# A list scheduler's prices for TensorE: new durations and a new charge for changes of tiling

## The chip, the cores and the metric

The kernel runs on one core of one Trainium2 chip. The metric is the device time of one execution in microseconds. One execution more was profiled; all durations below come from it. TensorE (PE) multiplies matrices, PEld is its loading of the stationary operand, DVE is VectorE, ACT is ScalarE, POOL is GpSimd, SP is SyncE, which issues the DMAs.

## The reference, cut to what matters

Four transformer layers on 512 tokens of width 1024, everything in float32. The first two layers each run four mixers side by side (a gated linear attention with 64-wide heads, `hgrn2`; one with 32-wide keys, `gla`; a causal softmax attention, `mla`; a gated delta rule, `gdn`) and then a feed-forward part with a gated, convolved projection. The last two are an attention layer with differences of softmaxes and a stick-breaking layer, both with a small attention over 256 memory tokens.

```python
def first_block(x, ...):
    for l in range(DEPTH):
        z = rms_norm(x, pre_mix_g[l]) @ w_in[l]            # 512 x 3256
        o_a = hgrn2_mixer(...)     # chunk_gla, chunks of 64, 4 heads of 64
        o_b = gla_mixer(...)       # chunk_gla, keys of 32
        o_c = mla_mixer(...)       # causal softmax
        o_d = gdn_mixer(...)       # chunk_gated_delta: triangular solve, then 8 chunks in sequence
        mix = jnp.concatenate([o_a, o_b, o_c, o_d], axis=-1) @ w_out[l]
        x = x + rms_norm(mix, post_mix_g[l])
        x = x + rms_norm(conv_glu_ffn(rms_norm(x, pre_ffn_g[l]), ...), post_ffn_g[l])   # 1024 -> 2816 -> 1024
    return x

def reference(...):
    return second_block(first_block(x, ...), ...)   # diff attention layer, stick-breaking layer
```

## The kernel before

The large products (projections, feed-forward, output projections) are done with float32 split into a high and a low `fp32r` part, three matmuls for one (`mm3`, L814). These are 128x128 tiles of the array with 256 to 512 moving columns, and they are called dense below. The small products of the mixers are plain float32: of 64 rows and 64 columns (K = 64, M = 64, n = 64) in `gdn` (L1540) and parts of `gla_core` (L1072), of 128 rows and 64 columns in the six levels of `gla_core`, a few with 32. A plain float32 matmul is two MATMUL instructions in the profile. In `gdn` they come in batches of 32 matmuls (`batch`, L1624) that read tiles which DVE or ACT has just written; the eight chunks in sequence come as groups of four.

No instruction is issued while the Python program runs. Every call of an engine is put down as an `Op` in a `Plan` (L261) with what it must follow, and `Plan.emit` (L324) issues them at the end in the order that `Plan.order` (L410) returns. This is why L328 is the line of every row of the profile. The order comes from a list scheduler, `Plan.simulate` (L422). It holds a clock for each engine. Whenever an engine is free on that clock it takes, of the ops that are ready, the one with the lowest rank (the place in which the Python program wrote it, as far as tiles suffice: `feasible`, L378), and moves the clock on by the op's price, `Plan.cost` (L330). A successor on another engine becomes ready at the end plus a hop (`HOP`). The start times of this simulation, sorted (L595), are the instruction order of every engine's queue and of the DMA queue. On the chip each queue then runs strictly in that order and waits on semaphores: prices only decide the order.

Four things in `simulate` touch PE alone:

- the price of a matmul by its type, K, M and n (L333 to L343);
- the tiling: if an op's pair of K and M, each cut off at 64, isn't that of the op before, 0.08 us are added (L555). By that cut, 128x128, 128x64 and 64x64 are one class;
- a guess of the TensorE clock: if too few columns were streamed in a period of the model, prices double in the next (`slow`, L500, L562);
- mixing (L505 to L534): if few columns have lately been streamed (`lately`, `MIX`, `CHUNK`), ops with `dense` below 0.9 are passed over as long as a denser one is ready. `dense` is an op's columns per ns of its price (L414), so a price can move an op over that bound.

All 8 PSUM banks are in three pools: `psA` for the projections, `psS` and `psD` for the mixers.

Of the kernel before, what the change touches and what calls it, by code (L numbers as in the profile page):

```python
# [164 lines left out]
class Clocks:  # L165
# [20 lines left out]
    def cost(self, e, kind, outs, ins):  # L186
        n = max(_free(a) for a in outs + ins)
        if e == "PE":
            if kind == "transpose":
                return 0.105  # L190
            n = _free(ins[-1])
            return max(0.055, n / 2400) if ins[-1].dtype == F32R else max(0.085, n / 600)
        if e == "ACT":
            return 0.2 + 0.83e-3 * n
        if e == "DVE":
            return 0.15 + (0.52e-3 if kind in ("tensor_scalar", "tensor_copy", "memset") else 1.04e-3) * n
        if e == "POOL":
            return 0.2 + 2.2e-3 * n
        return 2.5
# [61 lines left out]
class Plan:  # L261
# [68 lines left out]
    def cost(self, op):  # L330

        n = max([_free(a) for a in op.outs] + [_free(a) for a in op.ins])
        psum = any(a.tensor.name.startswith("ps") for a in op.ins)  # L333
        if op.eng == "PE":
            if op.kind == "transpose":
                return 0.11
            n = _free(op.ins[-1])
            if op.ins[-1].dtype == F32R:
                return 0.0025 + max(n, 256) / 2400
            M = op.outs[0].shape[0]  # L340
            if M > 64:
                return max(0.214, 0.002 + n / 600)
            return 0.0135 + n / 1200 if M <= 32 else max(0.081, 0.028 + n / 1200)  # L343
        if op.eng == "ACT":
            acc = 0.1 if op.kw.get("accum_out") is not None else 0.0
            ptr = any(hasattr(op.kw.get(k), "tensor") for k in ("scale", "bias"))
            return (0.05 if psum else 0.09) + 0.833e-3 * n + acc + (0.09 if ptr else 0.0)
        if op.eng == "DVE":
            if op.kind == "reciprocal":
                return 0.07 + 6.25e-3 * n  # L350
            if op.kind == "memset":
                return 0.01 + 1.042e-3 * n
            fast = op.kind in ("tensor_scalar", "tensor_copy") and not psum
            ptr = any(hasattr(op.kw.get(k), "tensor") for k in ("scalar", "scalar1", "scalar2"))
            return 0.07 + (0.521e-3 if fast else 1.042e-3) * n + (0.06 if ptr else 0.0)
        if op.eng == "POOL":
            if op.kw.get("op") == ALU.pow:
                return 0.3 + 0.165 * _free(op.outs[0])
            return 0.15 + (2.1e-3 if op.kind == "tensor_tensor" else 3.33e-3) * n
        return 0.45  # L360
# [4 lines left out]
    TABLES = {AF.Exp: "natural_log_exp_and_others", AF.Ln: "natural_log_exp_and_others", AF.Silu: "silu",  # L365
              AF.Sigmoid: "sigmoid", AF.Gelu_apprx_tanh: "gelu", AF.Sin: "sin"}
    TABLE_LOAD = 1.3

    WINDOW, COLUMNS = 10.24 / 3, 3060.0
    MIX, CHUNK = 1.2, 1000.0  # L370
# [48 lines left out]
    def hop(self, a, b):  # L419
        return self.HOP.get((a, b), 0.1)  # L420

    def simulate(self, rank, prio):  # L422
# [60 lines left out]
        indeg = [len(op.preds) for op in ops]  # L483
        at = [0.0] * len(ops)
        table, bw = None, 0.0
        cols, window, slow, boost, tiling = 0.0, 0, True, False, None
        recent, lately = collections.deque(), 0.0
        events = []
        for op in ops:
# [5 lines left out]
        while len(out) < len(ops):  # L495
            t, e = heapq.heappop(events)
            if clock[e] > t:
                continue
            while e == "PE" and t >= (window + 1) * self.WINDOW:
                slow = cols < self.COLUMNS  # L500
                cols, window = 0.0, window + 1
            while later[e] and later[e][0][0] <= t:
                _, n = heapq.heappop(later[e])
                heapq.heappush(ready[e], (prio[n], n))
            pick, skipped = None, []  # L505
            if e == "PE":
                while recent and recent[0][0] < t - self.WINDOW:
                    lately -= recent.popleft()[1]
                boost = lately < self.MIX * self.COLUMNS + (self.CHUNK if boost else 0.0)
            while ready[e]:  # L510
                p, n = heapq.heappop(ready[e])
                op = ops[n]
                wait, tag = None, None
                for nm in op.new:
                    tag = self.tags[nm][0]
                    if not free[tag] or not can(nm):
                        wait = math.inf
                        break
                    if free[tag][0] > t:
                        wait = free[tag][0]  # L520
                        break
                if wait is not None:
                    if wait < math.inf:
                        heapq.heappush(later[e], (wait, n))
                    else:
                        blocked.setdefault(tag, []).append(n)
                    continue
                if e == "ACT" and op.func in self.TABLES and self.TABLES[op.func] != table and at[n] + self.PATIENCE > t:
                    skipped.append((p, n))
                    continue  # L530
                if boost and op.dense < 0.9 and e == "PE":
                    skipped.append((p, n))
                    continue
                pick = n  # L534
                break
            if pick is None and skipped:
                pick = skipped.pop(0)[1]
            for x in skipped:
                heapq.heappush(ready[e], x)
            if pick is None:  # L540
                if later[e]:
                    heapq.heappush(events, (max(later[e][0][0], t + 1e-6), e))
                continue
            op = ops[pick]
            start = t
            wake = set()
            for nm in op.new:
                take(nm)
                wake.add(self.tags[nm][0])
            if e == "ACT" and op.func in self.TABLES and self.TABLES[op.func] != table:  # L550
                table = op.table = self.TABLES[op.func]
                start += self.TABLE_LOAD
            op.start = start
            if e == "PE":
                mode = min(op.ins[0].shape[0], 64), min(op.outs[0].shape[0], 64)  # L555
                cost = op.cost * (2 if slow else 1) + (0.08 if mode != tiling else 0.0)
                tiling = mode
                cols += self.columns(op)
                lately += self.columns(op)
                recent.append((start + cost, self.columns(op)))  # L560
                while start + cost >= (window + 1) * self.WINDOW:
                    slow = cols < self.COLUMNS  # L562
                    cols, window = 0.0, window + 1
            else:
                cost = op.cost
            clock[e] = end = start + cost
            if e == "DMA":
                n = 4e-6 * math.prod(op.outs[0].shape)
                bw = end = max(bw, start + 1.8) + n / 0.36
                end += 0.9  # L570
            op.end = end
            out.append(op)
            for nm in op.tiles:
                left[nm] -= 1
                tend[nm] = max(tend[nm], end)
                if not left[nm]:
                    drop(nm, tend[nm] + 0.15)
                    wake.add(self.tags[nm][0])
            for tag in wake:
                for n in blocked.pop(tag, ()):  # L580
                    f = ops[n].eng
                    heapq.heappush(later[f], (t, n))
                    heapq.heappush(events, (max(t, clock[f]), f))
            for s in op.succs + op.soft:
                f = ops[s].eng
                if s in op.succs:
                    at[s] = max(at[s], end + hop(e, f))
                else:
                    at[s] = max(at[s], start + 0.01)
                indeg[s] -= 1  # L590
                if not indeg[s]:
                    heapq.heappush(later[f], (at[s], s))
                    heapq.heappush(events, (max(at[s], clock[f]), f))
            heapq.heappush(events, (clock[e], e))
# [19 lines left out]
class Net:  # L614
# [256 lines left out]

    def fm(self, h, w, M=128):

        ps = self.ps("A")
        for k in range(KT):
            self.mm3(ps[:M], (w[0][:, k, :], w[1][:, k, :]), self.hp(h, k, 0, S), k == 0, k == KT - 1)
        return ps
# [66 lines left out]

    def w_fm(self, W, c0, M=128):
        return self.wload(self.cols(W, c0, M))

# [1576 lines left out]
```

## Time and profile before

| | us |
|---|---|
| three runs: median (lowest to highest) | 2035.56 (2032.98 to 2035.82) |
| the profiled execution: its time | 2033.99 |
| its span, first to last instruction | 2032.2 |
| PE busy in it | 1954.1 (96%) |
| DVE / ACT / POOL busy | 1250.3 / 946.6 / 265.7 |
| mean granted TensorE clock | 0.987 |

The stretches: mixers of the first layer from about 60 to 260 us, of the second from 784 to 984; feed-forward from about 380 to 735 and from 1100 to 1450; the attention layers from 1450 to the end. In a timeline row, start and length are in us, equal instructions that follow each other are merged (x is their number), and the brackets give the engine's idle time before them and what ended it. A length includes the way through the array, so rows overlap: the pace of a group is the distance of starts.

### The profile page before, as it was taken

How to read it: one execution, taken by the hardware profiler on the slowest of the kernel's cores; microseconds unless marked ns; L12 is line 12 of the kernel's file. 1: busy time of each engine (PE TensorE's matmuls, PEld its weight loads, DVE VectorE, ACT ScalarE, POOL GpSimd, SP SyncE). 2: the span in 40 equal slices, each digit the busy share in tenths (PEclk: the TensorE clock that was granted, in tenths of full speed). 3: DMA queues.
4: the chain of work that ended last, by engine and by line, in shares of the span. 5: the costliest groups of instructions: out<-in, count | busy, mean ns of one | idle time of the engine just before them, and what ended most of it. 6: DMA issues, size and time to landing. Idle time of an engine off the chain costs nothing.

```text
span 2032.2 us, 33173 instructions
## 1 busy us (share of the span) xinstructions
PE 1954.1 (96%) x13254; PEld 1655.6 (81%) x13254; DVE 1250.3 (62%) x2319; ACT 946.6 (47%) x1715; POOL 265.7 (13%) x362
## 2 busy tenths in 40 slices
PE   7999989899999989998898999999999999999999
PEld 6888778788888878887787888888899988888787
DVE  7688873544442257878836444422548886558796
ACT  5744463433332236633634333322446774457782
POOL 3101111000000021011201000000223220005131
PEclk9999989999999999999999999999999999999999
DMA  5321224433332433302243333324331213421121
GB/s 166 97 63 36 83 81 138 125 94 94 98 99 94 155 90 96 92 24 68 82 152 112 100 94 94 99 97 167 121 89 43 84 63 114 135 84 55 60 74 62
DMA packets 231305, 191.62 MB, mean 94 GB/s; under 512 B 22352, under 2 KB 201200, under 8 KB 231152
## 3 DMA queue, kind: packets, MB, share of 16 engines
q1 hardware_dynamic: 231152, 189.51, 30.4%
q8 instruction: 104, 1.70, 0.3%
q14 instruction: 49, 0.40, 0.1%
HBM read 174.28 MB, written 15.20 MB: 93 GB/s over the span
## 4 chain that ended last, share of the span: by engine, by line
PE 84%; DVE 7%; ACT 3%; POOL 2%; issue 2%; DMA 1%; SPq 1%; DVEq 0%; ACTq 0%; POOLq 0%
PE psA L328 63%; PE psS L328 12%; PE psD L328 9%; DVE p4w L328 5%; POOL st L328 2%; ACT p4w L328 1%; DVE p4p L328 1%; DVE wl L328 1%; SPq L328 1%; DVE p L328 1%; ACT wh L328 0%; DMA wr<-in_w_in_dram 0%; ACT p4p L328 0%; ACT p L328 0%; DVE p4h L328 0%
## 5 line engine op out<-in xcount | busy, mean ns | idle before, releaser
L328 PE MATMUL psA<-p4h,wh 128*128 128x512 f32 (+1 forms) x2144 | 627.9, 377 | 14.3 <-DVE p4h L328 7.1
L328 DVE TENSOR_TENSOR wl<-wr,wh 128x1024 fp32r<-128x1024 f32 (+6 forms) x304 | 349.0, 1152 | 413.7 <-ACT wh L328 408.4
L328 ACT CAST wh<-wr 128x1024 fp32r<-128x1024 f32 (+6 forms) x304 | 298.5, 990 | 465.2 <-PE psA L328 279.8
L328 PEld LDWEIGHTS psA<-p4h,wh 128*128 128x128 f32 x2144 | 393.5, 191 | 89.9 <-DVE p4h L328 8.3
L328 PE MATMUL psA<-p4h,wl 128*128 128x512 f32 (+1 forms) x1072 | 400.6, 374 | 0.0
L328 PE MATMUL psA<-wh,p4h 128*128 128x256 f32 (+1 forms) x1792 | 353.8, 289 | 0.9 <-DVE p4h L328 0.7
L328 PEld LDWEIGHTS psA<-wh,p4h 128*128 128x128 f32 x1792 | 282.3, 188 | 6.6 <-issue 2.0
L328 PE MATMUL psA<-wl,p4h 128*128 128x256 f32 (+1 forms) x896 | 257.5, 288 | 0.4 <-DVE wl L328 0.4
L328 PEld LDWEIGHTS psA<-p4h,wl 128*128 128x128 f32 x1072 | 204.3, 191 | 37.0
L328 POOL TENSOR_SCALAR st<-st 128x1 f32<-128x1 f32 (+4 forms) x108 | 46.1, 427 | 1310.6 <-ACT p4w L328 908.5
L328 PEld LDWEIGHTS psA<-wl,p4h 128*128 128x128 f32 x896 | 168.8, 188 | 2.6 <-DVE wl L328 0.8
L328 PE MATMUL psA<-wh,p4w 128*128 128x512 f32 (+1 forms) x540 | 159.4, 368 | 0.0
L328 ACT ACTIVATE p<-p 128x512 f32<-128x512 f32 (+2 forms) x174 | 87.3, 526 | 100.2 <-DVE p L328 98.9
L328 POOL TENSOR_TENSOR st<-st,c 128x1 f32<-128x1 f32 (+4 forms) x106 | 115.4, 1090 | 8.0
L328 ACT ACTIVATE p4w<-psA 128x256 f32<-128x256 f32 (+5 forms) x138 | 61.6, 452 | 107.0 <-PE psA L328 105.9
L328 PEld LDWEIGHTS psA<-wh,p4w 128*128 128x128 f32 x540 | 96.6, 188 | 18.2 <-issue 0.5
L328 PE MATMUL psS<-consts,p4w 128*128 128x128 f32 (+1 forms) x448 | 70.5, 291 | 36.7 <-DVE p4w L328 28.9
L328 PE MATMUL psS<-p4w,p4w 128*64 128x64 f32 (+9 forms) x800 | 94.6, 271 | 5.3 <-DVE p4w L328 5.1
L328 PE MATMUL psA<-wl,p4w 128*128 128x512 f32 (+1 forms) x270 | 98.5, 365 | 0.0
L328 PE MATMUL psS<-wh,p4w 128*128 128x512 f32 x300 | 97.3, 395 | 0.0
L328 DVE TENSOR_TENSOR p<-psA,p 128x512 f32<-128x512 f32 x54 | 37.3, 691 | 95.8 <-PE psA L328 94.2
L328 PEld LDWEIGHTS psS<-consts,p4w 128*128 128x128 f32 x448 | 54.5, 153 | 47.7 <-issue 19.1
(227 smaller groups left out, 3105.0 us busy)
## 6 DMA issues: line engine op xcount, KB each, us to landing
wr<-in_w_in_dram SPq DMA_DIRECT2D x44, 512.0 KB, 3.8
wr<-in_ffn_w_gate_dram SPq DMA_DIRECT2D x44, 512.0 KB, 3.8
wr<-in_ffn_w_up_dram SPq DMA_DIRECT2D x44, 512.0 KB, 3.8
wr<-in_ffn_w_down_dram SPq DMA_DIRECT2D x44, 512.0 KB, 3.5
wr<-in_w_out_dram SPq DMA_DIRECT2D x16, 512.0 KB, 4.7
wr<-in_a_w_in_dram SPq DMA_DIRECT2D x16, 512.0 KB, 3.8
wr<-in_b_w_in_dram SPq DMA_DIRECT2D x16, 512.0 KB, 3.9
p4w<-xd SPq DMA_DIRECT2D x12, 512.0 KB, 4.4
```

The costliest lines, as they stand in the source:

```text
L328: op.fn(*op.args, **op.kw)
```

## The change

Only `Plan` changes. The prices of PE's ops are replaced, the charge for a change of tiling becomes one that depends on the tiling that is left, and the tiling of an op is now told apart in 32, 64 and 128 for rows and columns. What is computed, the ranks, the pools and the prices of the other engines stay.

```diff
             if op.kind == "transpose":
-                return 0.11
+                return 0.109
             n = _free(op.ins[-1])
             if op.ins[-1].dtype == F32R:
-                return 0.0025 + max(n, 256) / 2400
-            M = op.outs[0].shape[0]
+                return max(0.109, 0.0015 + n / 2232)
+            K, M = op.ins[0].shape[0], op.outs[0].shape[0]
             if M > 64:
-                return max(0.214, 0.002 + n / 600)
-            return 0.0135 + n / 1200 if M <= 32 else max(0.081, 0.028 + n / 1200)
+                return max(0.22, n / 560)
+            if M > 32 and (K > 64 or n > 64):
+                return max(0.09, 0.03 + n / 1120)
+            return 0.045 if M > 32 else 0.0135 + n / 1120
...
+    DRAIN = {(128, 128): 0.095, (128, 64): 0.195}
+
+    @staticmethod
+    def tiling(op):
+        return tuple(128 if n > 64 else 64 if n > 32 else 32 for n in (op.ins[0].shape[0], op.outs[0].shape[0]))
...
-        cols, window, slow, boost, tiling = 0.0, 0, True, False, None
+        cols, window, slow, boost, tiling = 0.0, 0, True, False, (128, 128)
...
-                mode = min(op.ins[0].shape[0], 64), min(op.outs[0].shape[0], 64)
-                cost = op.cost * (2 if slow else 1) + (0.08 if mode != tiling else 0.0)
+                mode = self.tiling(op)
+                cost = op.cost * (2 if slow else 1) + (self.DRAIN.get(tiling, 0.142) if mode != tiling else 0.0)
```

## Rows read from the trace of the kernel before

**Rows 1.** The page's first part: busy us, share of the span, instructions, by engine.

```profile
PE 1954.1 (96%) x13254; PEld 1655.6 (81%) x13254; DVE 1250.3 (62%) x2319; ACT 946.6 (47%) x1715; POOL 265.7 (13%) x362
```

**Rows 2.** The chain that ended last: shares of the span by engine.

```profile
PE 84%; DVE 7%; ACT 3%; POOL 2%; issue 2%; DMA 1%; SPq 1%; DVEq 0%; ACTq 0%; POOLq 0%
```

**Rows 3.** Stretches: length, then busy us (instructions) by engine, granted clock, DMA.

```profile
60.00:260.00 200.00, 191.69 (x2337) 163.33 (x2336) 159.36 (x317) 105.17 (x186) 27.53 (x31) 0.99 0.27 73
784.00:984.00 200.00, 191.19 (x2332) 163.95 (x2331) 159.15 (x317) 104.33 (x185) 28.11 (x33) 0.98 0.26 73
1450.00:2015.00 565.00, 556.78 (x3675) 488.82 (x3673) 416.76 (x922) 348.05 (x727) 133.19 (x172) 1.00 0.26 80
...
380.00:735.00 355.00, 354.42 (x1564) 289.19 (x1563) 149.97 (x177) 116.48 (x155) 7.91 (x17) 1.00 0.34 104
```

**Rows 4.** Waits of PE, 60 to 260 us: total us, times, longest.

```profile
PE psS L328 <- DVE p4w L328: 5.2, 6, 1.3
PE psD L328 <- DVE p4w L328: 1.6, 2, 1.4
```

**Rows 5.** Timeline of PE: a batch of 32 small matmuls and the stall behind.

```profile
99.22 1.33 PE L328 MATMUL psD<-p4p,p4w 64*64 64x64 f32 x64
100.47 0.74 PE L328 MATMUL psA<-p4h,wh 128*128 128x512 f32 x2
...
103.54 1.25 PE L328 MATMUL psD<-consts,p4w 128*128 128x128 f32 x8 [1.41 <-DVE p4w L328]
```

**Rows 6.** Timeline of PE: dense, 72 small instructions, dense.

```profile
143.58 0.50 PE L328 MATMUL psA<-wh,p4h 128*128 128x256 f32 x2
...
144.04 0.39 PE L328 MATMUL psA<-wh,p4h 128*128 128x256 f32 x2
...
144.38 0.39 PE L328 MATMUL psA<-wh,p4h 128*128 128x256 f32 x2
...
145.15 0.80 PE L328 MATMUL psS<-p4p,p4w 64*64 64x64 f32 x37
...
145.81 1.30 PE L328 MATMUL psD<-p4w,p4w 64*64 64x64 f32 x33
147.05 0.50 PE L328 MATMUL psA<-wh,p4h 128*128 128x256 f32 x2
```

**Rows 7.** Timeline of PE in the second layer's mixers.

```profile
921.35 1.09 PE L328 MATMUL psS<-p4w,p 128*64 128x128 f32 x16 [2.76 <-DVE p4w L328]
922.37 0.51 PE L328 MATMUL psA<-wh,p4h 128*128 128x256 f32 x2
...
923.04 0.39 PE L328 MATMUL psD<-p4w,p4w 64*64 64x64 f32 x6
...
924.35 0.66 PE L328 MATMUL psS<-consts,p4w 128*128 128x128 f32 x4
...
929.56 0.32 PE L328 MATMUL psD<-p4w,p4w 64*64 64x64 f32 x2 [1.67 <-DVE p4w L328]
```

**Rows 8.** Timeline of PE in the feed-forward part.

```profile
500.12 0.62 PE L328 MATMUL psA<-p4h,wh 128*128 128x512 f32 x2
...
500.80 0.62 PE L328 MATMUL psA<-p4h,wh 128*128 128x512 f32 x2
```

**Rows 9.** Instructions by form, PE, whole span: busy us, mean ns, idle before.

```profile
L328 PE MATMUL psD<-p4w,p4w 64*64 64x64 f32 x1136 | 48.2, 224 | 4.8 <-DVE p4w L328 3.0 <-DMA p4w<-db 1.3 <-ACT p4w L328 0.3
...
L328 PE MATMUL psS<-p4w,p4w 128*64 128x64 f32 x384 | 15.1, 227 | 1.7 <-DVE p4w L328 1.6
```

**Rows 10.** The tile st: duration ns min/median/max of its instructions, forms.

```profile
L328 POOL TENSOR_SCALAR st<-st x108: 192/199/1346, 5.5 to 1855.1; 128x1 f32<-128x1 f32 x60, 128x16 f32<-128x16 f32 x12, 128x4 f32<-128x4 f32 x12, 128x8 f32<-128x8 f32 x12
L328 POOL TENSOR_TENSOR st<-st,c x106: 547/640/3979, 6.4 to 1855.5; 128x1 f32<-128x1 f32 x60, 128x4 f32<-128x4 f32 x12, 128x8 f32<-128x8 f32 x12, 128x2 f32<-128x2 f32 x12
```

**Rows 11.** A stretch at the lower clock in the mixers, columns as in Rows 3.

```profile
930.12:933.53 3.41, 3.41 (x61) 3.24 (x62) 1.68 (x3) 0.38 (x1) 0.00 (x0) 0.50 0.00 0
```

**Rows 12.** Waits of PE, 1450 to 2015 us.

```profile
PE psS L328 <- POOL p4w L328: 4.1, 5, 1.3
```

## The prediction

> **What bounds the kernel now.** I read the busy shares first: TensorE is busy for 96% of the span and the next engine, VectorE, for 62% [rows 1]. The chain that ended last says the same from the other side: 84% of it is PE, and VectorE is the only other engine with more than 3% [rows 2]. So the sum of PE's work sets the time, and the set of matmuls does not change. What an order can change is PE's idle time, its passages from one tiling to another, and its clock. The table of stretches tells where there is any: in the feed-forward stretch PE is busy for 354.42 of 355 us, so nothing can be won there; in the mixers it idles 200 - 191.69 = 8.3 us in the first layer and 200 - 191.19 = 8.8 us in the second; in the attention layers 565 - 556.78 = 8.2 us [rows 3]. The rest of its idle time, 2032.2 - 1954.1 = 78.1 less 25.3 and the half us of the feed-forward, so some 52 us, lies at the start, the end and the passages between parts, where a norm chain has no other work beside it in any order. I cost those at no change.
>
> In the mixers 6.8 us of the first layer's 8.3 end with a write of VectorE to a mixer tile [rows 4]. The reader should see two such stalls in the timelines: a batch of 32 small matmuls, three dense instructions and a few more, and then PE stands for 1.41 us until VectorE has written [rows 5]; in the other layer 70 small instructions, some dense, a stall of 1.67 us [rows 7]. A queue runs in the simulated order, so a stall means that the simulation thought the tile ready when PE came to it. It had PE's clock too late, or VectorE's too early.
>
> **The change part by part.** *Small matmuls, 64x64 with 64 columns.* Before, 0.081 us each: a batch of 32 was worth 2.59 us. On the chip it starts at 99.22 and dense work goes on at 100.47, 1.25 us with the passage into it [rows 5]. The simulation was 1.34 us late behind it, and the stall behind it is 1.41. The 70 instructions, 35 matmuls, were priced 2.84 and took from 923.04 to 924.35, 1.31 us: 1.5 late, and the stall is 1.67 [rows 7]. The new price is 32 x 0.045 + 0.095 + 0.142 = 1.68 for the batch, 0.43 over the chip. By the code there are nine such batches in `gdn`, three in the 64-wide `gla_core` and one in the other, 13 a layer; 1136 instructions of one of these forms alone stand in the trace [rows 9]. So 13 x 0.91 = 11.8 us of overpricing go from each layer.
>
> I take half of the mixers' idle time (17.1 us in both layers) to stand behind such batches, as the two stalls shown do, and 0.91 / 1.34 = 68% of that to go, because dense work is then sorted into the gap: 17.1 x 0.5 x 0.68 = 5.8 us won. The bounds are 0 (the gap is filled with work that a later gap then lacks) and 17.1.
>
> The Trainium skill, in "TensorE: Matmul & The Clock Gate" (section "Wait — 56ns, not 53.3ns?"), states that starts of matmuls never come closer than about 25 ns, however few the columns. The trace disagrees: 64 instructions in 1.25 us are 19.5 ns each, passage included [rows 5]. By the page a batch could not take less than 1.6 us, the overpricing would be 0.99 instead of 1.34, and as an estimate the 5.8 us would shrink to some 4.3.
>
> *Mixing.* A small op's density was 64 columns / 0.081 = 0.79, under the bound of 0.9, so a run of them was broken off in favour of dense ops. With 0.045 it is 1.42 and the run goes on. Such a cut shows: 72 instructions (36 matmuls) between two blocks of dense ones; the block before takes 145.15 - 143.58 = 1.57 us for 12 instructions whose pace is 0.34 us for three [rows 6]. That is 1.36, so a cut costs 0.21 us in two passages. I count about four a layer that look so; 8 x 0.21 = 1.7 us won. Bounds: 0 (the next batch waits for an evacuation and the passage comes all the same) and, with twice as many, 3.4.
>
> *128 rows, 64 columns wide (the levels).* Here the price goes the wrong way. Eight matmuls with 128 moving columns take 922.37 - 921.35 = 1.02 us [rows 7]; they were priced 1.08 and now 1.15 + 0.095 + 0.195 = 1.44. Sixteen with 64 columns take about 32 x 15.1 / 384 = 1.26 by busy time [rows 9]; they were 1.30 and become 1.73. So 0.4 us of new overpricing for each of 12 levels a layer, 24 in all: 9.6 us is the bound of what it can cost, 0 the other. The levels wait for VectorE as it is (2.76 us before one [rows 7]); I take 1.5 us lost.
>
> *Dense matmuls.* 512 columns: three take 0.68 us, 0.227 each [rows 8]; the price was 0.216 and is 0.231. 256 columns: 0.113 [rows 6], priced 0.109, now 0.116. Before, the simulation's PE ran 5% ahead in dense stretches, so an op that depends on VectorE or ScalarE was sorted behind more dense work than it needed: a lead. Now PE is 2 to 3% late and the lead is gone. In the feed-forward nothing depends on it. In the attention layers it can cost: bounds 0 and +16 (worked out below), of which I take 1.0, as PE's waits there are few.
>
> *Transposes* at 0.109 for 0.110 and the 32-wide forms change nothing that counts.
>
> The sum: -5.8 - 1.7 + 1.5 + 1.0 = -5.0 us. Against the profiled execution's 2033.99 that is 2029.0. The median of the three runs is 1.57 above it, so a median after the change may lie at 2030.5; I name 2029.
>
> **The rivals.** *The lead is lost and the attention layers pay (slower).* Place: 1450 us to the end. The mechanism: with exact or late PE prices every underpriced step of another engine becomes a stall. Such steps exist: POOL's two instructions of each norm are priced 0.153 and 0.465 and take 0.199 and 0.640 in the median [rows 10], 0.22 us too little, and the largest wait of these layers is for POOL already, 4.1 us in five stalls [rows 12]. Against it: ScalarE and VectorE still have a hop in every step, and 8.2 us idle in 565 is little. Price: if PE idles there at the mixers' rate, 17.1 us in 400, that is 24.2 us in 565, 16 more than now. With the mixers' gain of about 6, that makes 2034 + 10 = 2044; at two thirds of it, 2039. It outweighs the gain from about 5 us more idle time there, and is measurably slower from 9.
>
> *The order shifts and the time doesn't.* Ranks are unchanged and the scheduler takes the lowest that is ready; each gap filled takes dense work from a later one, and VectorE is busy 159 of 200 us in the mixers [rows 3], so the mixers may end when its chain ends. Then 2034, give or take 3. For it: the work in reserve is finite. Against: PE is busy for 96% there and has dense work until the end of the stretch.
>
> *The clock.* Small runs that are no longer cut may bring the lower clock. One of the three short stretches at 0.50 in the mixers begins behind the 1.67 us stall and among small matmuls [rows 7, 11]; 3.41 us at half the clock costs up to 1.7. Five more would take away the gain and bring 2029 + 8.5 = 2037.5; but shorter stalls should remove some.
>
> *All of the idle time goes:* 17.1 + 1.7 won, 2015.
>
> **How the numbers follow.** About 0.2% (4 us) is what a measurement of this kernel can tell from no change: faster means below 2031.5, slower above 2039.6. Chances: my forecast 0.45, all of the idle time 0.05, no effect 0.24, the lost lead 0.20, the clock 0.06. A forecast that comes out a little weaker falls in the same, and about a fifth of the two slower rivals' and of the no-effect case's weight spreads over the bounds: faster 0.50, same 0.24, slower 0.26. The range goes from near the all-gone case, 2017, to the full price of the lost lead, 2044; the forecast's own range is 2024 to 2033.
>
> **What would show it.** Right: in the mixers no stall over 1 us right behind a batch of 64x64 matmuls, runs of 64 instructions uncut, PE's idle time in the two stretches at about 11 us for 17; in the attention layers 8 to 10 us. Wrong: idle time there at 15 or more, stalls for POOL that have grown; or the mixers' stretches as long as before with their stalls in new places, in front of levels above all; or more than three short stretches at 0.50. The forecast fails above all if the gap of each stall is filled by work that is missing before the mixers' end.

## The result: slower by 1.1%

Median 2058.43 us (2056.32 to 2060.03, 4 runs) against 2035.69 us (2032.98 to 2036.67, 4 runs): ratio 1.0111, 95% interval 1.0095 to 1.0127. The forecast was 2029. The profiled execution took 2059.18 us, with a span of 2057.4 us, 25.2 more than before.

In the profile after, the busy shares and the same stretches of mixers and attention layers as in [rows 3] (the feed-forward stretch is busy throughout, 355.00 of 355 us):

```profile
PE 1963.2 (95%) x13254; PEld 1666.8 (81%) x13254; DVE 1248.6 (61%) x2319; ACT 945.9 (46%) x1713; POOL 263.3 (13%) x362
```

```profile
60.00:260.00 200.00, 187.67 (x2306) 163.13 (x2306) 158.36 (x316) 103.02 (x185) 28.89 (x35) 0.96 0.24 66
784.00:984.00 200.00, 186.27 (x2214) 162.03 (x2213) 155.23 (x311) 99.11 (x178) 27.89 (x33) 0.94 0.24 66
1450.00:2015.00 565.00, 549.52 (x3596) 481.19 (x3595) 403.38 (x896) 338.48 (x712) 130.18 (x175) 0.99 0.26 82
```

The same 13254 matmuls keep PE busy 9.1 us longer, and its idle time grows by 16.1, from 78.1 to 94.2. The idle time of the mixers went from 17.1 to 12.3 + 13.7 = 26.0 us, where the forecast had 11. The granted clock (the third column from the end) fell as well, from 0.99 and 0.98 to 0.96 and 0.94. It has two levels here, 1.00 and 0.50 (2.4 and 1.2 GHz). Adding up all stretches at the lower one gives 85.31 us, 70.93 of them busy (the sum row of such a table of 16 stretches):

```profile
sum 85.31, PE 70.93 PEld 64.03 DVE 68.25 ACT 31.88 POOL 7.05; mean PE 4.43 PEld 4.00 DVE 4.27 ACT 1.99 POOL 0.44
```

Before there were eight such stretches:

```profile
sum 51.20, PE 36.56 PEld 27.91 DVE 40.53 ACT 24.33 POOL 9.50; mean PE 4.57 PEld 3.49 DVE 5.07 ACT 3.04 POOL 1.19
```

At half the clock the difference in busy time costs, as an estimate, (70.93 - 36.56) / 2 = 17.2 us. So 16.1 of idle time and 17.2 of clock make 33.3, and the span grew by 25.2: some 8 come back. PE's sequence has 261 passages between tilings before and 202 after; at the prediction's 0.21 us for two, 59 fewer make some 6 of them, and the rest is not placed.

To place the loss I cut both traces at the same instructions (the first of a form that opens a part), so that each part holds the same work of PE. The rows are before and then after, in the order first mixers with their output projection, second mixers, first attention layer, second attention layer:

```profile
61.90:331.10 269.20, 254.54 (x2722) 215.57 (x2722) 200.59 (x396) 140.01 (x254) 38.11 (x44) 0.97 0.28 82
785.90:1054.90 269.00, 254.08 (x2721) 216.63 (x2721) 200.15 (x396) 138.71 (x252) 38.50 (x45) 0.97 0.28 82
1333.00:1724.00 391.00, 384.01 (x2492) 340.24 (x2491) 234.92 (x526) 187.63 (x378) 73.29 (x116) 1.00 0.31 98
1724.00:2022.00 298.00, 296.76 (x1715) 248.03 (x1714) 217.06 (x435) 186.60 (x384) 67.01 (x72) 1.00 0.23 73
```

```profile
61.70:334.60 272.90, 254.14 (x2721) 218.06 (x2721) 199.75 (x396) 140.54 (x254) 36.75 (x44) 0.96 0.28 83
789.90:1067.00 277.10, 256.57 (x2722) 221.48 (x2722) 199.95 (x396) 139.40 (x252) 38.11 (x45) 0.94 0.27 80
1345.00:1745.10 400.10, 387.51 (x2490) 343.20 (x2489) 234.06 (x526) 184.98 (x376) 73.44 (x116) 0.99 0.30 95
1745.10:2047.20 302.10, 299.21 (x1717) 248.01 (x1716) 217.37 (x435) 187.00 (x384) 66.36 (x72) 1.00 0.23 72
```

The second number is the length: +3.7 and +8.1 in the mixers, +9.1 and +4.1 in the attention layers, 25.0 in all.

Two places in the timeline of PE after show how. The stall that was forecast to go has gone: the batch of [rows 5] stands in two halves, with dense work where the 1.41 us were, and no idle time is printed:

```profile
98.84 1.15 PE L328 MATMUL psD<-p4p,p4w 64*64 64x64 f32 x32
99.92 0.51 PE L328 MATMUL psA<-p4h,wh 128*128 128x512 f32 x1
...
100.58 1.15 PE L328 MATMUL psD<-p4p,p4w 64*64 64x64 f32 x32
...
104.61 0.66 PE L328 MATMUL psD<-consts,p4w 128*128 128x128 f32 x4
```

But where the kernel before cut small work with dense work [rows 6], in the second layer after there is nothing but small work from 863.44 to 874.79, with a stall inside, then nineteen dense instructions and a stall of 3.04:

```profile
863.44 3.30 PE L328 MATMUL psD<-p4w,p4w 64*64 64x64 f32 x57
...
871.82 2.08 PE L328 MATMUL psD<-p4w,p4w 64*64 64x64 f32 x64 [1.61 <-DVE p4w L328]
873.83 1.03 PE L328 MATMUL psS<-p4w,p4w 128*64 128x64 f32 x26
874.79 0.39 PE L328 MATMUL psA<-wh,p4h 128*128 128x256 f32 x1
...
880.26 0.42 PE L328 MATMUL psS<-p4w,p4w 128*64 128x64 f32 x6 [3.04 <-DVE p4w L328]
```

Two stretches at the lower clock begin there, one at the start of the small run, one behind the second stall:

```profile
863.47:866.88 3.41, 3.41 (x73) 3.41 (x77) 2.03 (x4) 0.78 (x2) 0.00 (x0) 0.50 0.61 216
880.54:887.36 6.82, 6.82 (x108) 6.28 (x104) 3.03 (x5) 1.75 (x3) 0.00 (x0) 0.50 0.01 2
```

### The profile page after: what moved, and what is told of

The parts are those of the page before. It is cut to its first block, busy times and chain, and to the rows that moved or that the text cites. A ratio compares the mean times of both kernels' runs of the same rounds, so it can differ in the third digit from the quotient of the medians.

```text
span 2057.4 us, 33200 instructions
## 1 busy us (share of the span) xinstructions
PE 1963.2 (95%) x13254; PEld 1666.8 (81%) x13254; DVE 1248.6 (61%) x2319; ACT 945.9 (46%) x1713; POOL 263.3 (13%) x362
## 5 line engine op out<-in xcount | busy, mean ns | idle before, releaser
L328 PE MATMUL psA<-wh,p4h 128*128 128x256 f32 (+1 forms) x1792 | 348.9, 290 | 1.7 <-ACT p4w L328 1.0
L328 ACT ACTIVATE p<-p 128x512 f32<-128x512 f32 (+3 forms) x174 | 87.4, 526 | 108.9 <-DVE p L328 107.8
L328 PE MATMUL psS<-p4w,p4w 128*64 128x64 f32 (+9 forms) x800 | 101.3, 292 | 17.0 <-DVE p4w L328 13.7
L328 PEld LDWEIGHTS psA<-wh,p4w 128*128 128x128 f32 x540 | 97.7, 191 | 21.5 <-ACT p4w L328 3.3
```

The costliest lines, as they stand in the source:

```text
L328: op.fn(*op.args, **op.kw)
```

## The experiments

Two theories at first. *Mixing*: the small form's density crosses the bound of 0.9, its runs are no longer cut, dense work no longer covers the waits for VectorE, and the clock falls. *Lead*: the dense price, 7% higher, takes away the distance between a write and its reader in PE's queue. "Density from the old prices" below means this edit, with the prices of before in `old_cost`:

```diff
-            op.dense = self.columns(op) / op.cost / 1e3 ...
+            op.dense = self.columns(op) / self.old_cost(op) / 1e3 ...
```

All ratios are to the kernel before on the same chip, with 95% intervals.

**mix_old**: all of the change, density from the old prices.

> All of the change, but the density that decides on mixing is worked out with the old prices. Theory 'mixing' (the small 64x64 matmuls pass the density bound of 0.9, so runs of them are no longer cut and the clock falls): at most 2042 us, lower clock on about 50 us as before. Theory 'lead' (dense matmuls priced 7% higher take away the distance between a write and its reader in PE's queue, PE stalls, and the stalls bring the lower clock): 2052 to 2060, idle time as after the change (about 88 us).

2044.82 us, 1.0054 (1.0036 to 1.0071). Between what the two theories said, 3 us above the one and 7 below the other. PE idles 2043.2 - 1962.6 = 80.6 us, not the 88 of the lead theory. The mixers' parts (cut as above) are 266.7 and 267.9 us long, shorter than before; the attention layers stay at 400.3 and 301.2. So mixing is the loss in the mixers (15.4 us of profile), and something else that in the attention layers.

**only_mix**: the kernel before, density of the small form alone from 0.045.

```diff
+                small = op.kind == "matmul" and op.ins[-1].dtype != F32R and max(op.ins[0].shape[0], op.outs[0].shape[0], _free(op.ins[-1])) <= 64 and op.outs[0].shape[0] > 32
+                op.dense = self.columns(op) / (0.045 if small else op.cost) / 1e3
```

> The kernel before, but the density of the 64x64 matmuls alone worked out with 0.045; all prices old. Theory 'mixing': 2050 or more, more stretches at the lower clock in the mixers. Theory 'lead': within 4 us of 2035.

2049.66 us, 1.0084 (1.0058 to 1.0110), just short of the 2050. All prices are old, so this is density alone. Its timeline shows one run of 256 small instructions from 134.53 on, with three stalls inside and no dense matmul; the stretch from 138.07 to 141.48 and the one from 148.31 to 151.72 are at the lower clock:

```profile
134.81 1.10 PE L328 MATMUL psS<-p4p,p4w 64*64 64x64 f32 x59
138.66 3.38 PE L328 MATMUL psD<-p4w,p4w 64*64 64x64 f32 x62 [2.75 <-DMA p4w<-db]
...
146.27 1.15 PE L328 MATMUL psD<-p4w,p4w 64*64 64x64 f32 x32 [2.31 <-DVE p4w L328]
148.61 1.97 PE L328 MATMUL psD<-p4w,p4w 64*64 64x64 f32 x32 [1.19 <-DVE p4w L328]
```

**only_dense**: the kernel before, new dense price.

```diff
-                return 0.0025 + max(n, 256) / 2400
+                return max(0.109, 0.0015 + n / 2232)
```

> The kernel before with the new price of the dense (fp32r) matmuls alone. Theory 'lead': 2048 or more, with some 6 us more idle time in the first attention layer. Theory 'mixing': within 5 us of 2035.

2046.86 us, 1.0067 (1.0046 to 1.0088): 1 us short of the bound that the lead theory gave itself. The first attention layer has nearly the whole loss that it has in the changed kernel, 8.3 of 9.1 us, with 11.9 us idle for 7.0 before and two stretches at the lower clock, each right behind stalls:

```profile
1333.90:1733.20 399.30, 387.40 (x2489) 343.97 (x2488) 234.88 (x526) 185.00 (x376) 71.66 (x116) 0.99 0.30 96
```

**null**: the price of a transpose 0.109 for 0.11.

> The kernel before with the price of a transpose alone at 0.109 for 0.11. Theories 'mixing' and 'lead': within 3 us of 2035. A third theory, that any touch of a price shuffles the order and moves the time: 5 us or more away, either way.

2035.12 us, 1.0002 (0.9989 to 1.0014), although nearly 1700 of the 13254 places of PE's sequence hold a matmul of another form or tile. This shuffle moves the time less than 0.2%. The parts move more, and against each other: cut as above they are 266.0, 267.8, 392.6 and 297.7 us long, -3.2, -1.2, +1.6 and -0.3 against before. A difference of this size in one part says nothing by itself.

**mix_off**: the kernel before without mixing.

```diff
-    MIX, CHUNK = 1.2, 1000.0
+    MIX, CHUNK = 0.0, 0.0
```

> The kernel before with the mixing taken away altogether (its bound set to 0 columns), all prices old. Theory 'mixing' (cutting runs of small matmuls with dense ones covers the waits for ACT and DVE and keeps the clock up): 2046 or more, about as with the density of the small form alone raised. Theory that the raised density hurts by making small matmuls count as dense while mixing goes on: within 4 us of 2035.

2060.12 us, 1.0115 (1.0099 to 1.0132): 14 us above the bound of 2046, and 10 above only_mix. Mixing is worth 1.1% here; the mixers' parts grow to 280.0 and 281.0 us.

**scaled**: only_dense, and ACT, DVE, POOL and all hops 7% dearer.

```diff
-                cost = op.cost
+                cost = op.cost * (1.0 if e == "DMA" else 1.07)
...
-        return self.HOP.get((a, b), 0.1)
+        return 1.07 * self.HOP.get((a, b), 0.1)
```

> The kernel before with the new dense price, and with the prices of ACT, DVE and POOL and all hops 7% higher as well. Theory 'lead' (only the ratio of PE's prices to the other engines' decides, and that ratio had kept readers behind their writers): 2031 to 2039, idle time in the two attention layers back to 8 to 9 us. Theory that any move away from the old order's details costs, or that the dense price acts through the clock guess or the density: 2044 or more, as with the dense price alone.

2031.73 us, 0.9985 (0.9974 to 0.9997). The loss of the dense price alone is gone when the other engines' prices rise with it: here the price acts through the ratio. The attention layers idle 7.9 + 1.5 us, close to the 8 to 9 expected; the mixers' parts, 263.9 and 266.3 us, are a little shorter than before as well. The first attention layer is back:

```profile
1328.30:1719.80 391.50, 383.56 (x2489) 340.82 (x2489) 235.67 (x526) 187.42 (x378) 72.23 (x116) 1.00 0.30 98
```

**more_lead**: the dense price of before times 0.95.

> The kernel before with the dense price 5% lower still. Theory 'lead': 2030 to 2037, idle time in the attention layers at 8 us or less. Theory that the price of before was a lucky point: 2042 or more.

2034.12 us, 0.9991 (0.9982 to 1.0001). The time is as expected, but not the reason: the attention parts idle 11.7 us, not 8, and are 394.3 and 300.6 us long, 5.9 more than before; the mixers idle 21.5 us for 29.6. In the attention layers the dense price of before was a lucky point after all: a lower one loses there too, which the lead theory does not explain.

**keep_both**: the changed kernel with the dense price of before and density from the old prices.

> The change's prices of the plain float32 matmuls and its charges for tiling, but the dense price of before and the density worked out with the old prices. If mixing and the dense price are the two causes and they add: 2028 to 2034, the mixers some 3 to 4 us shorter each than before, the attention layers as before. If the small prices or the charges cost something of their own: 2038 or more.

2036.93 us, 1.0004 (0.9995 to 1.0014): no change, between the two expectations. The mixers win 5.7 us, the attention layers lose 6.5, with the old dense price. A third cost is left.

**repair**: all prices and charges of the change, density from the old prices, other engines and hops 7% dearer.

> All of the change's prices and charges, with both suspected causes undone in another way than before: the density worked out with the old prices, and ACT, DVE, POOL and the hops 7% dearer. If the causes are the density and the ratio of PE's prices to the others': 2026 to 2034, idle time in the attention layers 8 to 10 us. If the absolute dense price matters: 2042 or more.

2036.92 us, 1.0005 (0.9995 to 1.0014). Most of mix_old's loss is gone, but the time is 3 us above the range, and the first attention layer stays at 400.6 us with 13.3 idle, though the ratio of the dense price is restored.

**more_mix**: scaled, with MIX at 1.6.

> The dense price new, ACT, DVE, POOL and hops 7% dearer, and the bound of mixing at 1.6 for 1.2. If mixing wins by keeping the clock up and still has something to give: 2024 to 2030, less than 30 us of busy time at the lower clock. If 1.2 already does what can be done: 2029 to 2036.

2088.21 us, 1.0261 (1.0246 to 1.0277). Both expectations missed by 50 us. The mixers' parts take 295.7 and 290.8 us, idle 22 each, and the mean clock falls to 0.972. Of the three bounds run, 0, 1.2 and 1.6, the middle one is best; why 1.6 is so bad stays open.

**small_price**: the kernel before with the 64x64 matmuls at 0.045, density from the old prices.

```diff
+            if M > 32 and K <= 64 and n <= 64:
+                return 0.045
```

> The kernel before with the 64x64 matmuls priced 0.045, the density still from the old prices. If overpricing of these batches caused the mixers' stalls as predicted: idle time of the two mixers' parts 5 us or more below before's, time 2026 to 2031. If the stalls come back elsewhere: 2033 or more.

2017.77 us, 0.9912 (0.9897 to 0.9927). Better than both kernels, and 8 us below the range. The mixers' parts lose 9.7 and 8.4 us of length, and their idle time falls from 29.6 to 9.9 + 9.6:

```profile
61.50:321.00 259.50, 249.62 (x2722) 214.20 (x2722) 198.86 (x396) 139.43 (x254) 37.80 (x44) 0.97 0.29 85
776.60:1037.20 260.60, 250.96 (x2721) 217.07 (x2721) 198.69 (x396) 138.51 (x252) 38.83 (x45) 0.97 0.28 85
```

Where only_mix ran 256 small instructions with stalls, here the dense instructions stand between the batches, at their waits:

```profile
140.35 2.08 PE L328 MATMUL psD<-p4w,p4w 64*64 64x64 f32 x60
142.36 0.38 PE L328 MATMUL psA<-wl,p4h 128*128 128x256 f32 x1
142.58 0.28 PE L328 MATMUL psA<-wh,p4h 128*128 128x256 f32 x1
142.79 2.08 PE L328 MATMUL psD<-p4w,p4w 64*64 64x64 f32 x64
```

**only_drain**: the kernel before with the new charges alone.

> The kernel before with the new charges for a change of tiling alone. They make PE slower in the mixers only, by about 0.1 us at each of some 120 passages a layer: theory 'lead' says the mixers lose 2 to 6 us each to stalls, 2038 to 2046, the attention layers as before; theory that charges bring the order nearer to the chip's: 2028 to 2035.

2056.28 us, 1.0098 (1.0077 to 1.0118): beyond the 2046. The second mixers' part grows by 12.2 us, the first by 2.5, and the first attention layer by 5.3, though it has only six passages. The waits of PE from 790 to 990 us:

```profile
PE psS L328 <- DVE p4w L328: 6.4, 6, 3.8
PE psD L328 <- DVE p4w L328: 5.0, 3, 2.8
```

A passage does cost time on the chip (0.21 us for two in [rows 6]), but beside 0.081 for a small matmul, already above its pace, the charges overprice PE still more. For the first attention layer, with so few passages, that is no explanation.

Three runs more asked whether the charges and the dense price cost by making PE's clock late, or in some way of their own.

**small_drain**: small_price and only_drain together.

> The 64x64 matmuls at 0.045 (density from the old prices) and the new charges for tiling, nothing else. Theory 'overpricing' (what PE is priced above its pace in the mixers comes back as stalls, whichever term it is in): the price of a layer's small work falls by 17 us and rises by some 14, so 2026 to 2034. If the charges cost something of their own, the two effects add: 2036 to 2042.

2032.09 us, 0.9982 (0.9971 to 0.9993). In the range of overpricing, 4 us under the other. But adding the separate ratios (-0.88% and +0.98%) gives 2037, 5 us away, so the evidence is for overpricing and not strong.

**small_less**: small_price with 0.030.

> The 64x64 matmuls at 0.030, density from the old prices, nothing else: a batch of 32 is then priced 0.96 us, below its 1.25 on the chip. Theory 'overpricing': at or below the time with 0.045, 2008 to 2019. If 0.045 gained by being exact: 2022 or more.

2022.95 us, 0.9938 (0.9924 to 0.9953), in the range of the second theory by 1 us, 4 us outside the first. Going from 0.045 to 0.030 costs some 5 us, so a lower price is not better without end. With 0.045 a batch of 32 is priced 1.44 us; on the chip batches take from 1.25 us (the prediction's) to 2.01 (the rows of small_price above), so of the three prices run the one inside the chip's own spread is best.

**small_scaled**: small_price with the changes of scaled.

> The 64x64 matmuls at 0.045 (density from the old prices), the new dense price, and ACT, DVE, POOL and hops 7% dearer. Theory 'ratio' with additive gains: 2010 to 2018, and the attention layers within 3 us of before's. If the dense price costs by itself: 2024 or more.

2019.55 us, 0.9924 (0.9909 to 0.9938). 1.5 us over its range, 4.5 under the 2024: with the ratio kept, the dense price costs next to nothing, but scaled's small gain doesn't add. The first attention layer is 3.0 us longer than before.

A chain of runs gives each part's size in the place where it stands: small price -0.88%, then the charges +0.70 (small_drain), the other float32 prices +0.22 (keep_both), the dense price +0.50 (mix_old), the density +0.57 (the whole change). In us of 2035: -17.9 + 14.2 + 4.5 + 10.2 + 11.6 = +22.6. Each run of the chain starts from the one before it, so the sum closes by itself; each step is a difference of two ratios, good to some 3 to 5 us by their intervals. The steps depend on their place: alone, the charges cost 19.9 us, the dense price 13.6, the density 17.1.

## Why the prediction was wrong

The sum was -5.0 us and the chain of runs has +22.6. Two terms turned the sign: mixing, forecast at -1.7 and +11.6 in place, and the charges, whose passages outside the batches and levels stood in the sum at nothing and which cost +14.2. The dense price, +1.0 and +10.2, was too small.

*Stalls behind batches of small matmuls: right, and three times as large.* I had -5.8 us; the price alone, without its side effect on density, wins 17.9. The mixers' parts lost 10.1 us of idle time, so half of it for such stalls was too little. They also lost 8.0 us of busy time in the same work; 29 fewer passages, which my sum did not count, are some 3 of these by my own 0.21 for two, and the rest is not placed. My pace of 1.25 us for a batch came from one form and was given to all 13: in small_price's rows 60 and 64 small instructions take 2.01 us each to the next start (140.35 to 142.36, 142.79 to 144.80). For such batches 2.59 was 0.6 us too much, not 1.34, and 1.68 is not too much at all. (The side estimate of 4.3 us was also scaled wrongly: with an overpricing of 0.99 the rule of the 5.8 lets 0.91 / 0.99 = 92% go, 7.9 us. It was no term of the sum.)

*Mixing: wrong in sign; this is the first step that failed.* I wrote that a cut "costs 0.21 us in two passages" and took 1.7 us as won. The cut was worth more than it cost: dense work between small batches covers the time in which VectorE and ScalarE write the next batch's input, and there is less time at the lower clock. The profiles weigh the two, though no run separates them: from mix_old to the changed kernel, which differ in the density alone, PE's idle time grows from 80.6 to 94.2 us, 13.6 of the 14.2 us of span, and its busy time at the lower clock from 64.91 to 70.93 us, worth some 3. (In only_mix it is 11.0 us of idle time and some 7 of clock.) So 1.7 us won became 11.6 lost in place, most of it cover. I had the rows: the run of 72 instructions in [rows 6] stands between blocks of dense ones, and I priced the passages but not what goes on beside the dense block. The bound "0" for this edit excluded a loss without a reason. The clock rival (0.06) named the smaller half of it: it had five more stretches at the lower clock, and the whole change has eight more; but mix_old has five of these already, without the longer runs.

*Charges for tiling: the second step that failed, by the size of its term.* I counted them within the batches (0.095 + 0.142 each) and in the levels, and left out the small groups: some 120 passages a layer, before priced at 0 for all but the 32-wide ones, at 0.1 to 0.2 each. That is about 14 us of price a layer, and all that the small price takes away is 476 x 0.036 = 17 (13 batches of 32 and 15 groups of four). Net, PE got hardly cheaper in the mixers, and the cause of the forecast's gain was nearly cancelled: the charges cost 14.2 in place, against nothing in my sum. That is argued for the mixers only. From small_price to small_drain their parts grow by 6.3 us, and the attention layers, with 22 passages in all, by 5.3; why these do is open. The first attention layer in small_drain and in keep_both:

```profile
1322.80:1717.50 394.70, 384.58 (x2489) 341.05 (x2488) 235.46 (x526) 187.52 (x378) 73.03 (x116) 1.00 0.30 97
1328.60:1724.80 396.20, 385.09 (x2494) 340.55 (x2493) 238.32 (x530) 189.02 (x380) 73.00 (x116) 1.00 0.30 96
```

*Dense price: right mechanism, too small.* I took 1.0 of bounds 0 and 16, "as PE's waits there are few". It cost 10.2 in place (13.6 alone). Alone it acts in the attention layers: they grow by 8.3 and 3.5 us, and idle time there rises from 8.2 to 15.0 us in the same work. In place 6.0 us of the 10.2 are there, since keep_both, with the old dense price, has already lost 6.5. Few waits did not mean that the lead was not needed (scaled), though more of it did not help there either (more_lead). The rival "the lead is lost" named the place and +16 for a loss of all of it; the whole change lost 13.2 us of length there, about half of it without the dense price. And its witness was wrong: waits for POOL went from 4.1 us [rows 12] to 4.4, and the new idle time is spread over VectorE and ScalarE:

```profile
PE psS L328 <- POOL p4w L328: 4.4, 4, 1.9
PE psS L328 <- DVE p4h L328: 2.5, 2, 2.3
PE psS L328 <- DVE p4w L328: 1.5, 2, 0.8
...
PE psA L328 <- ACT p4w L328: 1.0, 1, 1.0
```

*Levels*: the higher price of the 128-row forms was not run by itself. With the full-width float32 price it makes the +0.22%, 4.5 us for the 1.5 forecast, good to some 3. The place fits: from small_drain to keep_both the mixers' parts grow by 6.1 us, the attention layers, where there are no levels, by 1.2. After the change the stall of 2.76 before a level in [rows 7] is gone, and one of 3.87 stands before the batch of small matmuls behind it:

```profile
928.02 1.09 PE L328 MATMUL psS<-p4w,p 128*64 128x128 f32 x16
929.05 0.45 PE L328 MATMUL psD<-p4w,p4w 64*64 64x64 f32 x8
933.36 2.14 PE L328 MATMUL psS<-p4w,p4w 64*64 64x64 f32 x57 [3.87 <-DVE p4w L328]
```

The rival that the order shifts and the time does not is refuted here by the change itself and by small_price; that a shuffle can leave the time alone, null shows.

Open: why the first attention layer takes 391 to 393 us in seven of the profiles and 394 to 401 in the others, with only_drain among the slower ones. One sign goes with it: three stalls of 0.6 to 1.2 us within 4 us stand in the same place in six of the ten slower ones (the changed kernel, mix_old, only_dense, only_drain, small_drain and repair) and in none of the seven. So the charges alone bring them, and the dense price alone does; how is not shown.

## What to carry to other kernels

In a simulated order look at the ratio of one engine's prices to the others' (only_dense against scaled; repair shows that it is not all): raising one engine's prices to the chip's pace while the others stay as they were can remove the distance that kept readers behind their writers. Prices that also feed a heuristic (here the density that decides on mixing) must be changed apart from it: the same 0.045 won 17.9 us as a price, and as a density, which it carries over the bound of 0.9 (by the price formulas no other form's crosses it), it lost 11.6 in place. And before costing the removal of an interruption at its passages, look at what the other engines do meanwhile.

## What the runs showed of the hardware that was not expected

Stalls can cost twice, but do not always. A cluster of three (0.81, 0.68 and 0.96 us within 4 us in the changed kernel, the rows below) stands in the first attention layer; in only_dense and mix_old, which have it too, the granted clock stood at 0.50 for 3.41 us right behind it (from 1647.80 and 1646.85 us), in the changed kernel and in small_drain it did not. Over the whole changed kernel, time at the lower clock grew by 34 us, and its estimated cost of 17.2 us is as large as the idle time that came with it. Runs no slower than before have some of it too: PE is busy at the lower clock for 39.75 us in null's profile and for 52.74 in keep_both's, for 36.56 before.

```profile
1657.29 0.63 PE L328 MATMUL psS<-consts,p4w 128*128 128x128 f32 x4 [0.81 <-DVE p4w L328]
...
1658.83 0.47 PE L328 MATMUL psS<-p4w,p4w 128*128 128x256 f32 x2 [0.68 <-DVE p4w L328]
1660.27 0.38 PE L328 MATMUL psA<-wh,p4h 128*128 128x256 f32 x1 [0.96 <-ACT p4w L328]
```

Small matmuls of one shape have two paces: 64 MATMUL instructions of 64x64 with 64 columns take 1.25 us in [rows 5] and 2.01 us in the rows of small_price, both at the full clock. What sets the pace is not shown.
